# Spreading the norm factors of the attention heads by a store and a broadcast load in place of two matmuls

## The chip, the core and the metric

The kernel runs on one core of one Trainium2 chip. The time of a run is what the device reports for that core, in microseconds (us); smaller is better. A run of the kernel before takes 2206.67 us (median of three: 2206.53, 2206.67 and 2206.71).

## What is computed

One layer of a diffusion backbone over 2048 latent tokens of width 1024, with 256 context tokens: an adaLN-modulated RMSNorm, one input projection, differential attention in four heads beside a Fourier mixing of the other channels, an output projection with a gated residual, then a second norm, a two-level router and a mixture of 32 SwiGLU experts. What the change touches is the end of the attention. For each head the two softmax maps are subtracted, multiplied with the values, and each token's 128 outputs of that head are divided by their root mean square:

```python
p = jax.nn.softmax(s, axis=-1)
a = p[:, :, 0] - lam * p[:, :, 1]
return jnp.einsum('bhqk,bkhv->bqhv', a.astype(v.dtype), v)
...
o = lax.map(block, qb)
o = jnp.moveaxis(o, 0, 1).reshape(b, n, N_DA_HEADS, DA_V_DIM)
o = rms_norm(o, g_subln) * (1.0 - lambda_init)
```

The factor of this norm is one number for each token and head.

## The kernel before

The stages follow one another on the core: modulation, input projection, Fourier part, attention (`stage_attn`, L494), then router and experts (`stage_moe`). Attention works on 64 query tiles of 128 tokens (four heads of 16), and pairs of tiles `g` = 0 to 31 (256 tokens) share the matmuls with the values.

The order of the work in `stage_attn` is written out by hand. Time is cut into 384 slots, six to a query tile, so twelve to a pair; `put(s, order, f, ...)` (L651) files a function call under a slot, and the calls are issued slot by slot, within a slot by `order`. Every engine then takes its own instructions in that order. In slot `s` of tile `i` stand:

- `score` (L533): four matmuls of queries and 768 keys (L547) into one of two PSUM buffers `s`; VectorE scales them into SBUF and takes a running minimum (L550).
- `transp` (L598) of a tile two and a third tiles back: three transposes on TensorE (L606) into one of three PSUM buffers `tp`, which ScalarE and VectorE split into a high and a low part (`split`: L98 ScalarE, L99 VectorE).
- `av` (L610) of an earlier pair: the products of weights and values, three matmuls each (L103 to L105); 18 calls of it are spread over ten of a pair's twelve slots.
- the softmax around it: `expo` on ScalarE (L562); the sums and their ratio, `weight` (L569 GpSimd, L573 and L575 VectorE); `scale` of the second map in three parts (L582 ScalarE, L586 GpSimd, L584 VectorE); the sum of the two maps, `weigh` on GpSimd, three instructions to a tile (L590).

The head's norm is `norm(g, step)` (L617). Below, `s0` = 12 `g` + 32 is the slot of step 0.

- Step 0, slot `s0`: ScalarE copies the 128x256 product out of PSUM into `o` (L622; dimensions on partitions, tokens along the row) and squares it (L624); GpSimd starts the factor tile `r` (128 tokens x 2) (L628).
- Step 1, slot `s0 + 4`: two matmuls of the squares with ones (L634) put each token's sum on that token's partition, VectorE adds it (L636), GpSimd takes the power -1/2 (L637).
- Step 2, slot `s0 + 6`: the factors have to stand along the row, on every partition. Two matmuls with the identity spread them (L641) into a third use of the `tp` buffers, VectorE multiplies (L644), and the SP queue stores the tile `m` into the DRAM tensor `S.mix` (L646), which the output projection reads later.

The SP queue issues most of the DMAs, in program order, and a DMA that waits holds up those behind it: the four loads of a pair's queries (`load_queries`, L773, issued at L778), the store of `m`, and, once for each of heads 1 to 3, the keys and values of the next head (`load_head`, L756, at L762 and L767) 18 slots ahead of the head.

Steps 1 and 2 of pair 29, and all of pairs 30 and 31, are issued by a second list (`DRAIN`, L998) after slot 383.

Of the kernel before, what the change touches and what calls it, by code (L numbers as in the profile page):

```python
# [10 lines left out]
F32 = mybir.dt.float32  # L11
# [4 lines left out]
OP = mybir.AluOpType  # L16
# [3 lines left out]
N, D, NC = 2048, 1024, 256  # L20
NT, ND = N // 128, D // 128
KT = (N + NC) // 128
H, DH, VD = 4, 64, 128
# [99 lines left out]
def bcast(ap, parts=128):  # L123

    return bass.AP(tensor=ap.tensor, offset=ap.offset, ap=[[0, parts]] + list(ap.ap))
# [368 lines left out]
def stage_attn(tc, A, S, G, kv, head, q0, late):  # L494
    nc = tc.nc
    NQ = N // 128
# [6 lines left out]
    W2 = 2  # L503
    NV = 10
    N1 = 4
    XO, TO, AO, LO = 4, 3, 5, 6
    SE = ("act", "pool", "dve")
    LV = 2
    SC = DH ** -0.5
    with ExitStack() as outer, ExitStack() as ctx:  # L510
        sm = outer.enter_context(tc.tile_pool(name="sm", bufs=4, reuse_waits="tile"))
        ep = outer.enter_context(tc.tile_pool(name="ep", bufs=2, reuse_waits="tile"))
        ps = outer.enter_context(tc.tile_pool(name="aps", bufs=2, space=PSUM, reuse_waits="tile"))
# [3 lines left out]
        wk = ctx.enter_context(tc.tile_pool(name="awk", bufs=2, reuse_waits="tile"))  # L517
# [99 lines left out]
        def norm(g, step):  # L617
            if step == 0:
                t = K()
                O[g, 1] = t  # L620
                t.o = wk.tile([128, 256], F32, name="o")
                nc.scalar.activation(t.o, O[g], AF.Copy)  # L622
                t.sq = wk.tile([128, 256], F32, name="sq", bufs=1)
                nc.scalar.activation(t.sq, t.o, AF.Square)  # L624
                t.r = sm.tile([128, 2], F32, name="r")
                for j in range(2):
                    s0 = ST[2 * g + j][:, 14:15]
                    nc.gpsimd.tensor_scalar(t.r[:, j:j + 1], s0, s0, VD * EPS, op0=OP.mult, op1=OP.mult)  # L628
                return
            t = O[g, 1]  # L630
            if step == 1:
                t.p = ps.tile([128, 2], F32, name="tp", bufs=3)
                for j in range(2):
                    nc.tensor.matmul(t.p[:, j:j + 1], t.sq[:, j * 128:(j + 1) * 128], G.ones[:, 0:1],  # L634
                                     start=True, stop=True)
                nc.vector.tensor_add(t.r, t.r, t.p)  # L636
                nc.gpsimd.tensor_tensor(t.r, t.r, G.mhalf.to_broadcast([128, 2]), op=OP.pow)  # L637
            else:
                t.p = ps.tile([128, 256], F32, name="tp", bufs=3)
                for j in range(2):  # L640
                    nc.tensor.matmul(t.p[:, j * 128:(j + 1) * 128], t.r[:, j:j + 1].to_broadcast([128, 128]),  # L641
                                     G.ident, start=True, stop=True)
                t.m = wk.tile([128, 256], F32, name="m", bufs=1)
                nc.vector.scalar_tensor_tensor(t.m, t.o, G.gsub, t.p, op0=OP.mult, op1=OP.mult)  # L644
                h, b = divmod(g, NQ // 2)
                nc.sync.dma_start(S.mix[h, :, b * 256:(b + 1) * 256], t.m)  # L646

# [3 lines left out]
        def put(s, order, f, *a):  # L651
            at_slot.setdefault(s, []).append((order, f, a))
# [26 lines left out]
        for g in range(H * NQ // 2):  # L679
            s0 = 2 * NS * g + NS + LT + LV  # L680
            for j in range(KT):
                put(s0 + j * NV // KT, AO, av, g, j)
            s0 += NV
            put(s0, 3.5, norm, g, 0)
            put(s0 + N1, 5, norm, g, 1)
            put(s0 + N1 + 2, 5, norm, g, 2)

        def early(t):
            if t == 0:
# [20 lines left out]
        i, g = H * NQ - 1, H * NQ // 2 - 1  # L710
# [1305 lines left out]
def mkconst(tc, const):  # L2016
    nc = tc.nc
    G = K()
    G.pool = const
    G.ident = const.tile([128, 128], F32, name="ident")  # L2020
    make_identity(nc, G.ident)
    G.ones = const.tile([128, 128], F32, name="ones")
    nc.vector.memset(G.ones, 1.0)
    G.mhalf = const.tile([128, 1], F32, name="mhalf")
    nc.vector.memset(G.mhalf, -0.5)
    G.total = const.tile([128, NE], F32, name="total")
    G.order = const.tile([1, NE], I32, name="order")
    G.over = const.tile([1, 2, OVMAX], I32, name="over")
    G.perm = const.tile([NE, NE], F32, name="perm")
    G.before = const.tile([NE, NE], F32, name="before")  # L2030
    G.two = const.tile([NE, 2], F32, name="two")
    G.rk = const.tile([NE, 1], F32, name="rk")
    G.lead = const.tile([1, 1], I32, name="lead")
    G.nover = const.tile([1, 1], I32, name="nover")
    return G


def body(tc, A, out):
    nc = tc.nc
    S = K()  # L2040

    def dram(name, shape, dt=F32):
        return nc.dram_tensor(name, shape, dt, kind="Internal").ap()

    S.q, S.k = dram("q", [2, H, 2 * DH, N]), dram("k", [2, H, 2 * DH, KT * 128])
    S.v = dram("v", [2, KT, 128, 512])
    S.mix = dram("mix", [ND, 128, N])
    S.fd, S.frow = dram("fd", [2, 128, 3, 2, 512]), dram("frow", [1, 2, 256 + H])
    S.mod = dram("mod_rows", [1, 4 * D])
    S.x1, S.h2 = dram("x1", [N, D]), dram("h2", [N, D])  # L2050
    S.hold = dram("hold", [1, 1])
    S.list = dram("list", [NE * ROWS, 2], I32)
    with tc.tile_pool(name="const", bufs=1) as const:
        G = mkconst(tc, const)
        late = ExitStack()
        late.manual = late.enter_context(ExitStack())
        with tc.tile_pool(name="kv", bufs=1, reuse_waits="tile") as kv:
            with tc.tile_pool(name="ada", bufs=1) as ada, ExitStack() as top:
                pa = top.enter_context(tc.tile_pool(name="pa", bufs=1, space=PSUM, reuse_waits="tile"))
                P = Spectra(tc, A, S, kv)  # L2060
                first = top.enter_context(ExitStack())
                first.enter_context(tc.manual_schedule())
                x0 = stage_ada(tc, A, G, ada, pa, P)
                with tc.tile_pool(name="win", bufs=1, reuse_waits="tile") as wp, \
                        tc.tile_pool(name="raw", bufs=2, reuse_waits="tile") as raw:
                    P.wp = wp
                    P.mid = ada.tile([128, 2, 4, 2, H], F32R, name="mid")
                    P.manual = late.manual
                    stage_in(tc, A, S, G, wp, raw, P, first, x0)
                    top.close()  # L2070
                    head, q = stage_fourier(tc, A, S, G, wp, P)
            stage_attn(tc, A, S, G, kv, head, q, late)
        with late:
            stage_moe(tc, A, S, G, late, out)
    return S, G
# [34 lines left out]
```

## Time and profile before

| | us |
|---|---|
| median of three runs | 2206.67 |
| the profiled execution | 2205.05 |
| its span, first to last instruction | 2203.4 |
| one pair of query tiles (12 slots) in the steady part of attention | 20.34 |

The span is what the trace's clock counts from; all times of rows below are from its start. Attention lies at 473 to some 1165 us. Its pairs repeat with a period of 20.34 us; the steps from one L644 to the next have this length to 0.03 us from the second pair on, up to the drain.

How to read rows: PE is TensorE's matmuls, PEld its loading of weights (each matmul has one, and the loads run ahead beside the matmuls), DVE VectorE, ACT ScalarE, POOL GpSimd, SP the queue that issues DMAs. `out<-in` names tiles, `L12` is a line of the kernel. A bracket at the end of a timeline row tells how long the engine was idle before the instruction and whose result ended that.

### The profile page before, as it was taken

The numbers are of one execution on the slowest core, as the hardware profiler recorded it, in microseconds if no ns is written. First come the engines' busy times: TensorE is split into PE (matmuls) and PEld (weight loads), VectorE is DVE, ScalarE is ACT, GpSimd is POOL, SyncE is SP. The second block draws the span as 40 slices with busy tenths as digits, with TensorE's granted clock in tenths as the row PEclk, the third lists the DMA queues.
The fourth block names the chain that finished last, engine by engine and source line by source line (L and its number), as shares of the span: only waits on it lengthen the run. The fifth ranks groups of instructions, "written<-read, shape, count | busy, mean of one in ns | idle before, by whom it ended". The sixth has DMA issues, their size and how long they took to land. (4 is left out here: it accounts for less than half of the span.)

```text
span 2203.4 us, 35346 instructions
## 1 busy us (share of the span) xinstructions
PE 2091.4 (95%) x12607; PEld 1823.4 (83%) x12607; DVE 1813.7 (82%) x3644; ACT 1381.8 (63%) x2385; POOL 1016.9 (46%) x817
## 2 busy tenths in 40 slices
PE   6999999998999999999999999899999999999991
PEld 2877888778999999999988888888888888888871
DVE  5766654479999999999987878689888998989885
ACT  3734444258788888888872222466767767676663
POOL 2211121127787878888772433423444434544223
PEclk9999999999999999999999999999999999999996
DMA  7566543482151141243125443799999999999986
GB/s 261 202 199 204 187 142 112 169 230 36 30 117 37 41 106 37 50 100 111 28 87 172 153 137 128 250 291 311 311 312 317 317 325 322 319 322 309 316 301 278
DMA packets 265679, 423.02 MB, mean 192 GB/s; under 512 B 23618, under 2 KB 120904, under 8 KB 263706
## 3 DMA queue, kind: packets, MB, share of 16 engines
q1 hardware_dynamic: 240714, 362.91, 50.3%
q0 software_dynamic: 15872, 39.67, 7.1%
q10 hardware_dynamic: 8912, 18.14, 2.2%
q8 instruction: 100, 1.64, 0.3%
q14 instruction: 81, 0.66, 0.1%
HBM read 342.42 MB, written 84.17 MB: 194 GB/s over the span
## 5 line engine op out<-in xcount | busy, mean ns | idle before, releaser
L1703 DVE TENSOR_TENSOR wl<-mraw,wh 128x1024 fp32r<-128x1024 f32 x382 | 472.7, 1273 | 8.1 <-ACT wh L1699 8.0
L1699 ACT ACTIVATE wh<-mraw 128x1024 fp32r<-128x1024 f32 x384 | 382.4, 1049 | 74.0 <-DMA mraw<-in_w_up_dram 37.0
L550 DVE TENSOR_SCALAR_CACHE_REDUCE e<-s 128x768 f32<-128x768 f32 x384 | 364.7, 950 | 24.3 <-PE s L547 24.1
L590 POOL TENSOR_TENSOR e<-e,e 128x768 f32<-128x768 f32 x189 | 359.4, 1929 | 5.4 <-DVE e L584 0.5
L562 ACT ACTIVATE e<-e,st 128x1152 f32<-128x1152 f32 x256 | 320.3, 1251 | 11.1 <-DVE st L556 7.6
L1767 PE MATMUL mu<-mxt,wh 128*128 128x320 f32 (+2 forms) x1024 | 281.2, 354 | 0.9 <-DVE sg L1776 0.6
L1768 PE MATMUL mu<-mxt,wl 128*128 128x160 f32 (+2 forms) x1024 | 246.0, 240 | 0.0
L98 ACT ACTIVATE ath<-tp 128x384 fp32r<-128x384 f32 x384 | 186.2, 486 | 72.4 <-PE tp L606 70.8
L99 DVE TENSOR_TENSOR atl<-tp,ath 128x384 fp32r<-128x384 f32 x384 | 210.9, 550 | 2.2 <-ACT ath L98 2.0
L1847 POOL DMA_INDIRECT x<-my,idx x46 | 105.0, 2283 | 206.3 <-DVE my L1837 199.7
L1768 PEld LDWEIGHTS mu<-mxt,wl 128*128 128x128 f32 x1024 | 195.6, 191 | 0.7
L1767 PEld LDWEIGHTS mu<-mxt,wh 128*128 128x128 f32 x1024 | 192.2, 188 | 2.4 <-DVE sg L1776 0.9
L606 PE MATMUL tp<-ident,e 128*128 128x128 f32 x1152 | 188.1, 273 | 1.2 <-DVE e L595 1.2
L547 PE MATMUL s<-kB,q 128*128 128x384 f32 x768 | 170.8, 344 | 5.8 <-DVE e L550 5.8
L1730 POOL DMA_INDIRECT mx<-h,idx x48 | 62.9, 1311 | 217.2 <-DMA idx<-list 131.1
L606 PEld LDWEIGHTS tp<-ident,e 128*128 128x128 f32 x1152 | 149.2, 140 | 15.0 <-issue 1.6
L547 PE MATMUL s<-kA,q 128*128 128x384 f32 x672 | 150.4, 345 | 9.3 <-DVE e L550 9.2
L547 PEld LDWEIGHTS s<-kB,q 128*128 128x128 f32 x768 | 125.6, 188 | 9.1 <-DVE e L550 9.1
L547 PEld LDWEIGHTS s<-kA,q 128*128 128x128 f32 x672 | 110.3, 189 | 13.2 <-DVE e L550 13.1
L586 POOL TENSOR_TENSOR e<-e,st 128x896 f32<-128x896 f32 x63 | 105.9, 1681 | 27.9 <-DVE st L575 24.3
L118 POOL TENSOR_SCALAR ss<-ss 128x1 f32<-128x1 f32 x18 | 10.9, 607 | 232.7 <-ACT junk L116 224.1
L103 PE MATMUL py<-wh,mah 128*128 128x512 f32 (+1 forms) x264 | 106.6, 404 | 0.2
(517 smaller groups left out, 5703.1 us busy)
## 6 DMA issues: line engine op xcount, KB each, us to landing
mraw<-in_w_gate_dram SPq DMA_DIRECT2D x64, 1024.0 KB
mraw<-in_w_up_dram SPq DMA_DIRECT2D x64, 1024.0 KB
mraw<-in_w_down_dram SPq DMA_DIRECT2D x64, 1024.0 KB
raw<-in_w_ada_dram SPq DMA_DIRECT2D x16, 1024.0 KB
q<-q SPq DMA_DIRECT2D x120, 128.0 KB
v<-z SPq DMA_DIRECT2D x18, 512.0 KB
k<-z SPq DMA_DIRECT2D x18, 512.0 KB
boot<-in_w_ada_dram SPq DMA_DIRECT2D x8, 1024.0 KB
```

The costliest lines, as they stand in the source:

```text
L98: nc.scalar.activation(hi, src, AF.Copy)
L99: nc.vector.tensor_sub(lo, src, hi.bitcast(F32))
L103: nc.tensor.matmul(out, ah, bh, start=start, stop=False)
L547: nc.tensor.matmul(p[:, u, :hw], q[:, m, x, qs], kvt.k[m][:, k0:k0 + hw], start=x == 0, stop=x == 1)
L550: nc.vector.tensor_scalar(E[i][m][:, c * CH:(c + 1) * CH].rearrange("p (u k) -> p u k", u=2), p[:, :, :hw], -SC, None, op0=OP.mult, op1=OP ...
L562: nc.scalar.activation(e, e, AF.Exp, scale=-1.0, bias=st[:, 6 + m:7 + m], accum_out=st[:, 8 + 2 * u + m:9 + 2 * u + m])
L590: nc.gpsimd.tensor_add(E[i][0][:, ks], E[i][0][:, ks], E[i][1][:, ks])
L606: nc.tensor.transpose(p[:, u, :], E[i][0][:, k0:k0 + 128], G.ident)
L1699: nc.scalar.activation(W.h[:, us, :], W.raw[:, us, :], AF.Copy)
L1703: engine.tensor_sub(W.l[:, us, :], W.raw[:, us, :], W.h[:, us, :].bitcast(F32))
L1767: nc.tensor.matmul(p[:, i, :2 * n], h, B.t[:, d, :], start=d == 0, stop=False)
L1768: nc.tensor.matmul(p[:, i, :n], l, B.t[:, d, :n], start=False, stop=d == ND - 1)
```

## The change

For pairs 0 to 27 (`g < LATE`) the factors take another way. Step 1 stores `r` into a new DRAM tensor `S.rn` (256 factors, by token) and loads that row back into a tile `m` on all 128 partitions, both on the SP queue. Step 2 stands at `s0 + 15`, nine slots later than before, has no matmuls, and multiplies `o` with `m` in place. The tile `o` has three buffers in place of two. Pairs 28 to 31 are computed as before.

```diff
@@ -503,6 +503,8 @@
     W2 = 2
     NV = 10
     N1 = 4
+    N2 = 11
+    LATE = H * NQ // 2 - 4
     XO, TO, AO, LO = 4, 3, 5, 6
     SE = ("act", "pool", "dve")
     LV = 2
@@ -618,7 +620,7 @@
             if step == 0:
                 t = K()
                 O[g, 1] = t
-                t.o = wk.tile([128, 256], F32, name="o")
+                t.o = wk.tile([128, 256], F32, name="o", bufs=3)
                 nc.scalar.activation(t.o, O[g], AF.Copy)
                 t.sq = wk.tile([128, 256], F32, name="sq", bufs=1)
                 nc.scalar.activation(t.sq, t.o, AF.Square)
@@ -635,13 +637,20 @@
                                      start=True, stop=True)
                 nc.vector.tensor_add(t.r, t.r, t.p)
                 nc.gpsimd.tensor_tensor(t.r, t.r, G.mhalf.to_broadcast([128, 2]), op=OP.pow)
+                if g < LATE:
+                    t.m = wk.tile([128, 256], F32, name="m", bufs=1)
+                    nc.sync.dma_start(S.rn[g].rearrange("(j p) -> p j", j=2), t.r)
+                    nc.sync.dma_start(t.m, bcast(S.rn[g]))
             else:
-                t.p = ps.tile([128, 256], F32, name="tp", bufs=3)
-                for j in range(2):
-                    nc.tensor.matmul(t.p[:, j * 128:(j + 1) * 128], t.r[:, j:j + 1].to_broadcast([128, 128]),
-                                     G.ident, start=True, stop=True)
-                t.m = wk.tile([128, 256], F32, name="m", bufs=1)
-                nc.vector.scalar_tensor_tensor(t.m, t.o, G.gsub, t.p, op0=OP.mult, op1=OP.mult)
+                if g < LATE:
+                    factors = t.m
+                else:
+                    factors = ps.tile([128, 256], F32, name="tp", bufs=3)
+                    for j in range(2):
+                        nc.tensor.matmul(factors[:, j * 128:(j + 1) * 128],
+                                         t.r[:, j:j + 1].to_broadcast([128, 128]), G.ident, start=True, stop=True)
+                    t.m = wk.tile([128, 256], F32, name="m", bufs=1)
+                nc.vector.scalar_tensor_tensor(t.m, t.o, G.gsub, factors, op0=OP.mult, op1=OP.mult)
                 h, b = divmod(g, NQ // 2)
                 nc.sync.dma_start(S.mix[h, :, b * 256:(b + 1) * 256], t.m)
 
@@ -683,7 +692,7 @@
             s0 += NV
             put(s0, 3.5, norm, g, 0)
             put(s0 + N1, 5, norm, g, 1)
-            put(s0 + N1 + 2, 5, norm, g, 2)
+            put(s0 + N1 + (N2 if g < LATE else 2), 5, norm, g, 2)
 
         def early(t):
             if t == 0:
@@ -2046,6 +2055,7 @@
     S.v = dram("v", [2, KT, 128, 512])
     S.mix = dram("mix", [ND, 128, N])
     S.fd, S.frow = dram("fd", [2, 128, 3, 2, 512]), dram("frow", [1, 2, 256 + H])
+    S.rn = dram("rn", [H * N // 256, 256])
     S.mod = dram("mod_rows", [1, 4 * D])
     S.x1, S.h2 = dram("x1", [N, D]), dram("h2", [N, D])
     S.hold = dram("hold", [1, 1])
```

## Rows read from the trace of the kernel before

**Rows 1.** Page of the profile, part 1: busy time, share of the span, instructions.

```profile
PE 2091.4 (95%) x12607; PEld 1823.4 (83%) x12607; DVE 1813.7 (82%) x3644; ACT 1381.8 (63%) x2385; POOL 1016.9 (46%) x817
```

**Rows 2.** Busy time by stretch: length, engines, PEclk (granted clock), DMA share, GB/s.

```profile
541.90:562.30 20.40, 17.19 (x114) 16.28 (x112) 19.61 (x51) 13.42 (x25) 11.15 (x13) 0.92 0.02 7
...
806.60:827.00 20.40, 20.04 (x148) 19.40 (x148) 19.50 (x51) 17.69 (x34) 16.43 (x14) 1.00 0.11 33
```

**Rows 3.** Waits, 600 to 1100 us: total us, times, longest.

```profile
DVE e L550 <- PE s L547: 20.7, 75, 0.3
```

**Rows 4.** Timeline of PEld, 819 to 842 us: start, us, engine, instruction.

```profile
819.87 0.65 PEld L547 LDWEIGHTS s<-kA,q 128*128 128x128 f32 x4 [0.57 <-DVE e L550]
...
823.79 0.65 PEld L547 LDWEIGHTS s<-kA,q 128*128 128x128 f32 x4
...
824.82 0.53 PEld L641 LDWEIGHTS tp<-ident,r 128*128 128x128 f32 x4
...
825.62 0.66 PEld L547 LDWEIGHTS s<-kA,q 128*128 128x128 f32 x4
...
832.59 0.66 PEld L547 LDWEIGHTS s<-kA,q 128*128 128x128 f32 x4
...
833.98 0.66 PEld L547 LDWEIGHTS s<-kA,q 128*128 128x128 f32 x4
...
840.21 0.65 PEld L547 LDWEIGHTS s<-kA,q 128*128 128x128 f32 x4 [0.57 <-DVE e L550]
```

**Rows 5.** Timeline of DVE, 800 to 842 us.

```profile
817.36 1.12 DVE L584 TENSOR_SCALAR e<-e,st 128x768 f32<-128x768 f32 x1
...
818.87 0.94 DVE L550 TENSOR_SCALAR_CACHE_REDUCE e<-s 128x768 f32<-128x768 f32 x1
...
820.21 0.94 DVE L550 TENSOR_SCALAR_CACHE_REDUCE e<-s 128x768 f32<-128x768 f32 x1
...
821.55 0.14 DVE L556 TENSOR_REDUCE st<-st 128x1 f32<-128x3 f32 x1
...
825.88 0.22 DVE L575 SCALAR_TENSOR_TENSOR st<-st,lam 128x1 f32<-128x1 f32 x1
...
826.48 0.47 DVE L644 SCALAR_TENSOR_TENSOR m<-o,gsub,tp 128x256 f32<-128x256 f32 x1
...
826.87 0.15 DVE L556 TENSOR_REDUCE st<-st 128x1 f32<-128x3 f32 x1
...
827.81 0.62 DVE L584 TENSOR_SCALAR e<-e,st 128x768 f32<-128x768 f32 x1
```

**Rows 6.** Timeline of POOL, short windows, so that nothing is merged.

```profile
816.38 1.68 POOL L586 TENSOR_TENSOR e<-e,st 128x896 f32<-128x896 f32 x1
...
820.12 1.83 POOL L590 TENSOR_TENSOR e<-e,e 128x768 f32<-128x768 f32 x1
...
826.18 1.68 POOL L586 TENSOR_TENSOR e<-e,st 128x896 f32<-128x896 f32 x1 [0.79 <-DVE st L575]
```

**Rows 7.** Timeline of DVE in the drain: two operands in SBUF.

```profile
1135.10 3.21 DVE L595 SCALAR_TENSOR_TENSOR e<-e,st,e 128x768 f32<-128x768 f32 x1
```

**Rows 8.** Timeline of POOL beside it, short windows.

```profile
1135.11 2.38 POOL L1050 TENSOR_TENSOR kB<-kA,e 128x1024 fp32r<-128x1024 f32 x1
...
1137.45 3.10 POOL L1050 TENSOR_TENSOR kB<-kA,e 128x1024 fp32r<-128x1024 f32 x1
```

**Rows 9.** Timeline of the SP queue: start, us to issue.

```profile
605.62 19.77 SPq L778 DMA_DIRECT2D q<-q  x4
...
1154.25 0.38 SPq L1066 DMA_DIRECT2D vA<-in_g_ffn_norm_dram  x1
...
1163.41 2.82 SPq L646 DMA_DIRECT2D mix<-m  x2
```

**Rows 10.** Timeline of DVE where it waits for such DMAs.

```profile
1159.78 1.23 DVE L1068 TENSOR_TENSOR kA<-kA,vA 128x1024 f32<-128x1024 f32 x1 [2.85 <-DMA vA<-in_g_ffn_norm_dram]
...
1165.39 0.48 DVE L644 SCALAR_TENSOR_TENSOR m<-o,gsub,tp 128x256 f32<-128x256 f32 x1 [0.81 <-DMA mix<-m]
```

## The prediction

> **What bounds the kernel now.** I read the page's busy times first: TensorE is busy 95% of the span, VectorE 82%, ScalarE 63%, GpSimd 46% [rows 1]. That is a mean over stages, so the next view was the busy time by stretch, around the lines that change. In a pair of the steady part (20.40 us) the weight loads fill 19.40 us and VectorE 19.50 us at a granted clock of 1.00, with the DMA engines at 11% [rows 2]: two engines lie within a hair of each other, and neither is the bound by its share alone. Which one ends waits has to be read in order of time.
>
> The timeline of weight loads shows the loop. TensorE stands still once in a pair, 0.57 us, for VectorE's L550, and starts the next slot's scores at 819.87; the same happens at 840.21, so a pair is 20.34 us [rows 4]. From 819.87 to the scores at 832.59 TensorE never waits for 0.1 us or more, and in that stretch VectorE waits for it: 20.7 us of such waits in the 500 us from 600 to 1100, which is 24.6 pairs, so 0.84 us per pair [rows 3]. After 832.59 VectorE runs without such a wait, through the L584 that takes 1.12 us (its counterpart of this pair starts at 817.36 [rows 5]), up to the L550 whose end lets TensorE go at 840.21. The loop of one pair is thus 12.7 us of TensorE and some 7.6 us of VectorE. What is taken from TensorE between 819.87 and 832.59 shortens it, if VectorE keeps up there; what is taken from TensorE elsewhere only lengthens its 0.57 us.
>
> **The change, part by part.**
>
> *The two matmuls go (L641).* They start at 824.82, inside TensorE's part of the loop. A slot that holds them and one value product takes from 823.79 to 825.62, 1.83 us; one with a value product and no L641 takes from 832.59 to 833.98, 1.39 us [rows 4]. So 0.44 us per pair. The third use of the `tp` buffers goes too; no wait for such a buffer stands in the steady pairs, so I cost that at nothing. There are 28 changed pairs. In the first, TensorE has time over: in the start-up stretch the weight loads fill 16.28 of 20.40 us and VectorE 19.61 [rows 2]. That leaves 27 pairs.
>
> *The product moves nine slots (L644).* It leaves the place where it took 0.39 us of VectorE's time (826.48 to the L556 at 826.87) and goes ahead of the L556 that starts at 821.55 [rows 5]. Both places lie in TensorE's part of the loop, so VectorE's own part keeps its length. Two things change beside the place.
>
> First, its second operand was in PSUM and is now in SBUF like the first. The nearest rows of a product with two operands in SBUF beside a busy GpSimd are in the drain: L595 on 768 columns, started at 1135.10, took 3.21 us and ended at 1138.31, which is 0.82 us after the GpSimd instruction started at 1135.11 had ended (1137.49); the GpSimd instruction behind that took 3.10 us in place of 2.38 [rows 7, 8]. So the product waits for the GpSimd instruction in progress, gets in at its end, and holds up the next one. At the new place GpSimd runs L590 from 820.12 to 821.95 [rows 6]: the product comes at 821.55, waits 0.40 us, and then runs 256/768 of the 0.82, some 0.27 us; it ends at 822.22 and, with the 0.08 us that neighbours overlap (0.47 us long, 0.39 us apart [rows 5]), takes 0.59 us of VectorE's time. The ends are 0.39 (no block) and 2.05 (a whole L590 of 1.83 us first). I take 0.59 because the phase is rigid: both the L590 and VectorE's path to 821.55 run without waits from the end of the L584 that started at 817.36, which itself ends 0.42 us after GpSimd's L586 (818.48 against 818.06 [rows 5, 6]).
> The Trainium skill, "SBUF — State Buffer", section "Who interferes with whom", has this as a rule and it speaks against the change: a VectorE instruction with two SBUF inputs and a GpSimd instruction that reads SBUF exclude each other, and the later one blocks until the earlier has ended; one with a single SBUF input does not contend. The rows of the drain agree. Without that rule the product would cost 0.39 and the sum below would be the same, since TensorE's part sets it.
>
> Second, at the old place less lies between L575 and L584. L586 on GpSimd starts when L575 is done and holds till 827.86 (826.18 and 1.68 [rows 6]); L584, now 0.39 us earlier, comes at 827.42 and, by the 0.42 us above, ends at 828.28 and not at 828.43 [rows 5]. So 0.15 of the 0.39 is won there.
>
> *VectorE's account.* It gets 0.59 and gives 0.15, so 0.44 more per pair, in a stretch that shrinks by 0.44: it needs 0.88 us of slack and has 0.84 of waits plus the tail of about 0.08 that each of its three waits hides. Between 0.00 and 0.04 us per pair is lost; I take 0.43 us won of the 0.44. This is a tie: every further tenth on VectorE costs a tenth of the pair.
> The later L556 delays ScalarE's exponential behind it by some 0.6 us; ScalarE idles 2.7 us of the pair [rows 2], and the splits behind it are due later on VectorE too, so I cost that at nothing.
>
> *The two DMAs (SP).* The factors are there by 824.82, where L641 read them, and the product now wants them at 841.89 (821.55 and a period): 17.1 us. A store of 128 KB issued at 1163.41 let its buffer go at 1165.39, 2.0 us; a broadcast load of 512 KB, issued at 1154.25, was waited for until 1159.78, 5.5 us with what lay ahead of it [rows 9, 10]. The store of the factors is smaller (1 KB, though in single elements) and the load is 128 KB, so 7.5 us is an upper price and 0 the lower, both under cover; if the cover is gone, VectorE stands. The load also waits for the one buffer `m`, free some 2 us after the previous product, so about when the store has landed. Behind these waits on SP stand the next head's loads and, nine slots later than before, the store of `m` and the four query loads; the queries are used a full pair later, and nothing reads `S.mix` before the drain. The tightest place is a head's load, three times: there the four query loads took 19.77 us to issue, to 625.39 [rows 9]. The factors' store now stands behind them: 625.4 and 7.5 make 632.9, and the product of that pair is due at 638.5 (602.74, 623.08 and so on are the old places, and the new one is 15.4 us behind). 5.6 us are left. The third buffer of `o` costs no instruction.
>
> **The sum.** 27 pairs by 0.43 us make 11.6 us. The profiled execution is 2205.05 us, so it becomes 2193.4; the median of the runs shown is 1.6 us above it, and I carry the difference over: 2206.67 - 11.6 = **2195.1 us**. The stages behind start when attention ends and move up as a whole; nothing of them was under way before.
>
> **Rivals.**
> *VectorE takes over.* If the blocked product or the shifted L584 costs 0.1 to 0.35 us more than above, the pair is VectorE's and 0.08 to 0.33 us are won: 2198 to 2204, some 2201. For: the tie. Against: VectorE's busy time counts overlaps, so its true slack is somewhat larger.
> *The saving is swallowed.* If TensorE waits as much longer elsewhere (its 0.57 us grows to 1.0), as in the first pair [rows 2], the time stays at 2206, give or take 2. Against: L641 lies in the unbroken stretch.
> *The port turns it round.* If GpSimd's third L590 gets in ahead of the product, or the product comes just behind 821.95, it waits through another L590 of 1.83 us: VectorE is 1.8 us over its tie and the pair becomes 19.9 + 1.8 = 21.7, 1.4 us longer than now, by 27: 2244 us. It decides from about 0.45 us of further waiting on, where the won 0.43 is gone. For: the skill's rule says that the block lasts for the whole instruction. Against: in the drain the product got in between two GpSimd instructions that stood back to back [rows 7, 8].
> *The factors land late.* From 17.1 us for both DMAs on, VectorE waits in every pair; at a head's load from 13.1 us on, three times. The second costs a few us, 2198 to 2200.
>
> **How the numbers follow.** The forecast has 0.62, VectorE taking over (with late factors at the heads) 0.15, the swallowed saving 0.10, the port or late factors in every pair 0.13. A measurement of this kernel can tell 0.2%, 4.4 us. Faster by more holds the forecast and three quarters of the second case: 0.73; slower 0.14, of which 0.01 is from the third case; the rest, 0.13, is the same. The range begins at 28 pairs by 0.44 with 1.5 us of scatter, 2192, and takes in the second case and the near part of the third up to 2205, which leaves some 0.2 out.
>
> **What would show it.** Right: a period of 19.9 us from product to product; no L641 ahead of pair 28; L644 some 0.7 us long, starting 0.4 us before a GpSimd L590 ends, and that engine's next L590 about 0.3 us longer; the L584 of the slot behind L575 at 0.85 in place of 0.62; no wait of L644 for a DMA; PE's wait for L550 still near 0.57. Wrong: L644 of 2 us or more, a DMA as its releaser, VectorE without waits for scores, or a period of 20.3.

## The result, and the profile after

The changed kernel takes 2226.09 us (median of six runs, 2220.8 to 2236.6) against 2206.69 us before: a ratio of 1.0095, 95% interval 1.0081 to 1.0108. It is slower by some 19 us, where 2195.1 was forecast. The profiled execution after took 2226.60 us, 21.6 us more than the one before. In attention, the 28 pairs from the 37th slot to the 373rd grow from 574.4 to 595.2 us together, so 20.8 us of the loss lie there.

Line numbers move: L644 is now L653, L547 is L549, L550 is L552, L575 is L577, L584 is L586, L590 is L592; the store of the factors is L642, their load L643, the store of the product L655.

**The steady pairs do what was forecast.** Two rows of the weight loads, as in [rows 4]:

```profile
663.42 0.65 PEld L549 LDWEIGHTS s<-kB,q 128*128 128x128 f32 x4 [0.57 <-DVE e L552]
...
683.30 0.65 PEld L549 LDWEIGHTS s<-kB,q 128*128 128x128 f32 x4 [0.56 <-DVE e L552]
```

The distance is 19.88 us in place of 20.34, and TensorE's one wait is still 0.56 to 0.57 us. On VectorE, the product and the L586 behind L577, which answer to [rows 5]:

```profile
684.98 0.69 DVE L653 SCALAR_TENSOR_TENSOR m<-o,gsub,m 128x256 f32<-128x256 f32 x1
...
691.00 0.86 DVE L586 TENSOR_SCALAR e<-e,st 128x768 f32<-128x768 f32 x1
```

The product is 0.69 us long (0.47 before), the L586 0.86 (0.62 before). GpSimd beside them, which answers to [rows 6]:

```profile
683.56 1.83 POOL L592 TENSOR_TENSOR e<-e,e 128x768 f32<-128x768 f32 x1
...
685.35 2.02 POOL L592 TENSOR_TENSOR e<-e,e 128x768 f32<-128x768 f32 x1
```

The product comes at 684.98, 0.41 us before the L592 ends at 685.39, and the next L592 takes 2.02 in place of 1.85 us. So it waits for the instruction in progress, gets in at the seam, and holds up the next by 0.17 us.

**The loss stands at three places.** The waits of VectorE, and of the SP queue, over attention (us in total, times, longest), which answer to [rows 3]:

```profile
DVE e L552 <- PE s L549: 5.5, 22, 0.7
...
DVE m L653 <- DMA m<-rn: 28.5, 3, 10.1
...
SPq L643 <- DMA rn<-r: 217.2, 28, 10.3
```

VectorE waits 5.5 us for scores, 23.7 us in the same stretch before, so it is now nearly the bound itself, the tie of the prediction. The product waits for its factors only three times, 28.5 us together: in pairs 4, 12 and 20, whose step 1 follows the load of the next head's keys and values. The last line says why it is not one or two us: in each of the 28 pairs the load of the factors waits 7.8 us on average for their store. The SP queue at the first head (start, time to issue), in the place of [rows 9]:

```profile
599.52 0.54 SPq L642 DMA_DIRECT2D rn<-r  x1
...
607.69 0.33 SPq L643 DMA_DIRECT2D m<-rn  x1
...
608.11 1.24 SPq L771 DMA_DIRECT2D kB<-k  x2
...
609.44 1.09 SPq L776 DMA_DIRECT2D vB<-v  x1
...
616.39 13.51 SPq L655 DMA_DIRECT2D mix<-m  x1
...
630.03 2.53 SPq L787 DMA_DIRECT2D q<-q  x4
...
633.00 0.38 SPq L642 DMA_DIRECT2D rn<-r  x1
...
640.49 0.33 SPq L643 DMA_DIRECT2D m<-rn  x1
```

Here is the chain. The factors' store of pair 3 is issued at 599.52, and their load waits for it until 607.69. Only then can the head load go, at 608.11; before it went at 603.66. Behind its 4.7 MB stands, new, the product's store of pair 3: it comes at 616.39 and takes 13.51 us to issue. Behind it the queries of the next pair, the first of the new head, and behind those, at 633.00, the factors' store of pair 4, whose load can go 7.5 us later, at 640.49. Two engines are late by it:

```profile
636.26 1.62 PE L549 MATMUL s<-kB,q 128*128 128x384 f32 x4 [2.75 <-DMA q<-q]
...
644.41 0.48 DVE L653 SCALAR_TENSOR_TENSOR m<-o,gsub,m 128x256 f32<-128x256 f32 x1 [8.80 <-DMA m<-rn]
```

The product of pair 4 could have started at 635.6 and stands 8.80 us. TensorE stands first for something else: the new head's first scores start 2.75 us late, for want of their queries (2.7 and 2.1 us at the other two heads). VectorE, which needs these scores, stands longer still for its factors, so the late queries cost nothing here; but they are a second thing that the block makes late. TensorE then computes two slots of scores and stands again until VectorE goes on. Its clock falls. Busy time by stretch (length; PE, PEld, DVE, ACT, POOL; granted clock; DMA share, GB/s), in the place of [rows 2]:

```profile
636.00:644.00 8.00, 7.27 (x30) 6.90 (x30) 0.00 (x0) 0.49 (x1) 1.68 (x1) 0.57 0.07 18
...
645.00:665.00 20.00, 18.75 (x124) 18.03 (x124) 18.81 (x46) 17.20 (x32) 14.06 (x12) 0.91 0.22 40
...
665.00:685.00 20.00, 19.65 (x144) 19.01 (x144) 19.80 (x50) 17.23 (x33) 16.53 (x14) 1.00 0.21 41
```

TensorE had stood 2.75 us for the queries; in the 8 us behind that its granted clock is 0.57, so mostly the lower of its two levels, 1.2 GHz, in the pair behind 0.91, and then 1.00, the upper one of 2.4 GHz, again. The account of the 28 pairs: the three stalled ones are 28.5, 29.8 and 29.4 us long and those behind them 20.9, 21.4 and 21.6, together 29.7 us above six pairs of 20.34; the 20 undisturbed ones win 20 by 0.45 or 9.0. That makes 20.7 of the 20.8 us.

### The profile page after: what moved, and what is told of

The parts are those of the page before. It is cut to its first block, busy times and chain, and to the rows that moved or that the text cites. A ratio compares the mean times of both kernels' runs of the same rounds, so it can differ in the third digit from the quotient of the medians.

```text
span 2225.0 us, 35210 instructions
## 1 busy us (share of the span) xinstructions
PE 2092.3 (94%) x12495; PEld 1823.6 (82%) x12495; DVE 1820.9 (82%) x3644; ACT 1368.8 (62%) x2385; POOL 1016.7 (46%) x817
## 5 line engine op out<-in xcount | busy, mean ns | idle before, releaser
L552 DVE TENSOR_SCALAR_CACHE_REDUCE e<-s 128x768 f32<-128x768 f32 x384 | 363.0, 946 | 8.5 <-PE s L549 6.7
L592 POOL TENSOR_TENSOR e<-e,e 128x768 f32<-128x768 f32 x189 | 360.0, 1932 | 5.4 <-DVE e L586 0.5
L549 PE MATMUL s<-kB,q 128*128 128x384 f32 x768 | 174.4, 349 | 19.2 <-DVE e L552 14.3
L549 PE MATMUL s<-kA,q 128*128 128x384 f32 x672 | 152.4, 349 | 17.1 <-DVE e L552 14.3
L549 PEld LDWEIGHTS s<-kB,q 128*128 128x128 f32 x768 | 128.2, 192 | 22.8 <-DVE e L552 19.9
L549 PEld LDWEIGHTS s<-kA,q 128*128 128x128 f32 x672 | 111.8, 191 | 21.4 <-DVE e L552 18.4
```

Of the source, the lines that this page charges most:

```text
L549: nc.tensor.matmul(p[:, u, :hw], q[:, m, x, qs], kvt.k[m][:, k0:k0 + hw], start=x == 0, stop=x == 1)
L552: nc.vector.tensor_scalar(E[i][m][:, c * CH:(c + 1) * CH].rearrange("p (u k) -> p u k", u=2), p[:, :, :hw], -SC, None, op0=OP.mult, op1=OP ...
L592: nc.gpsimd.tensor_add(E[i][0][:, ks], E[i][0][:, ks], E[i][1][:, ks])
```

## The experiments

**Head pairs as before.** Pairs 4, 12 and 20 go back to the two matmuls.

```diff
+        def spread(g):
+            return g < LATE and g % 8 != 4
...
-                if g < LATE:
+                if spread(g):
...
-            put(s0 + N1 + (N2 if g < LATE else 2), 5, norm, g, 2)
+            put(s0 + N1 + (N2 if spread(g) else 2), 5, norm, g, 2)
```

> Pairs 4, 12 and 20, whose step 1 falls behind the load of the next head, spread their factors by the two matmuls again, two slots after step 1; all other pairs as in the changed kernel. If the loss is the three waits of the product for its factors (8.8 to 10.1 us each, with a slower pair behind each), it is gone: the three pairs take 20.3 us, the other pairs stay at 19.9, and the run takes 2206.7 - 23 x 0.45 = 2196, between 2194 and 2199. If the head loads only hand the wait on to the pair behind (5, 13, 21), or the loss is one of the later stages, it stays above 2206.

Measured: 2245.18 us, ratio 1.0176 (1.0158 to 1.0193): worse than the changed kernel. That is above the 2206 of the second expectation, but not for its reason: no wait went to pairs 5, 13 and 21. The SP queue and VectorE at the first head:

```profile
619.73 13.98 SPq L658 DMA_DIRECT2D mix<-m  x1
...
633.83 2.53 SPq L790 DMA_DIRECT2D q<-q  x4
```

```profile
617.82 1.88 DVE L656 SCALAR_TENSOR_TENSOR m<-o,gsub,m 128x256 f32<-128x256 f32 x1 [0.54 <-DMA m<-rn]
...
639.14 0.48 DVE L656 SCALAR_TENSOR_TENSOR m<-o,gsub,tp 128x256 f32<-128x256 f32 x1 [14.95 <-DMA mix<-m]
```

The product of pair 3 comes at 617.82, and its store takes 13.98 us to issue behind the head load. Pair 4's product, early again, needs the one tile `m` that this store still reads, and stands 14.95 us (14.4 and 13.2 us at the other two heads). So taking away the two small DMAs behind the head load isn't enough: what the move has put behind the head load is the product's store of the pair ahead. The experiment was confounded by the single buffer, which I had left out of account.

**Clear of the heads.** The same edit, with the pair ahead of each head load taken out too:

```diff
+            return g < LATE and g % 8 not in (3, 4)
```

> Pairs 3, 4, 11, 12, 19 and 20 keep the two matmuls and the early product; the other 22 are spread. The order on SP around the three head loads is then that of the kernel before. The steady gain alone is left: no wait of a product over 2.5 us, the spread pairs at 19.9 us, and 2206.7 - 21 x 0.45 = 2197, between 2195 and 2200. If the gain of the steady pairs is given back in the experts' stage or in the drain, it stays above 2203.

Measured: 2196.81 us, ratio 0.9954 (0.9937 to 0.9970), as expected. No product waits for a store or a load of factors in the loop, and pair 3 stores its product ahead of the head load again:

```profile
603.02 0.33 SPq L658 DMA_DIRECT2D mix<-m  x1
...
603.39 1.71 SPq L774 DMA_DIRECT2D kB<-k  x2
```

It differs from the experiment above only in pairs 3, 11 and 19 (and 27, which no head load follows, so 21 pairs are spread, not 22). The 48 us between the two are theirs: a factors' store that the head load waits for, a store of the product that slides behind the head load, and the one buffer behind that. What is left against the kernel before is the gain of the pairs away from the heads.

**Head pairs alone.** The reverse: only pairs 4, 12 and 20 are spread.

```diff
+            return g in (4, 12, 20)
```

> Only pairs 4, 12 and 20, the three whose products waited, are spread by store and load; all others are as in the kernel before. So no factors' store stands ahead of the head load on SP, and no product's store between the head load and the queries: the head load starts near 603.7 us and the four query loads are issued by 625.5, as before. If the order on SP made the loss, the factors' store is issued at 625.5 and lands in 8 us, the load in 4: 637.5 against 638.5 us where the product is due, a wait under 1.5 us in each of the three, and attention as long as before to 4 us. If a head load and two small DMAs do not fit together in any order, the three waits are 8 to 10 us again and the run is some 30 us slower than before.

Measured: 2209.29 us (one run), beside 2207.68 before, and the 28 pairs take 577.7 us in place of 574.4. SP and VectorE at the first head:

```profile
605.19 1.22 SPq L774 DMA_DIRECT2D kB<-k  x2
...
607.15 19.88 SPq L790 DMA_DIRECT2D q<-q  x4
...
627.12 0.54 SPq L645 DMA_DIRECT2D rn<-r  x1
...
636.17 0.34 SPq L646 DMA_DIRECT2D m<-rn  x1
```

```profile
640.30 1.75 DVE L656 SCALAR_TENSOR_TENSOR m<-o,gsub,m 128x256 f32<-128x256 f32 x1 [0.66 <-DMA m<-rn]
```

The head load goes at 605.19, the queries directly behind it, as before the change, and the factors' store at 627.12: with the old order on the queue the factors land 0.66 us late in place of 8.80. So the order on SP makes about eight of the nine us, and the first expectation holds: the three waits are 0.66, 0.45 and 0.44 us. Both changes of the order count. From the start of the same slot, the 73rd, the head load goes 5.8 us later here and 11.6 us later in the changed kernel, where it has to wait for the factors' store of pair 3; and from the head load to the factors' store of pair 4 it is 21.9 us here and 24.9 us there, with the product's store between. The product is 1.75 us long here: it came at 640.30, 0.36 us after an L592 of 1.84 us had started on GpSimd, and ended 0.27 us after it. That is the price of a missed seam.

**The head load in two.**

```diff
-            KV[h], values = load_head(nc, S, kv, h)
-            values()
+            KV[h], V[h] = load_head(nc, S, kv, h)
+
...
+        def next_values(h):
+            V[h]()
...
-            put(h * NQ * NS - 3 * NS, 0, next_head, h)
+            put(h * NQ * NS - 5 * NS, 0, next_head, h)
+            put(h * NQ * NS - 3 * NS, 0, next_values, h)
```

> All pairs spread by store and load; a head's keys are loaded 30 slots ahead of it and its values 18, in place of both 18 slots ahead. If what hurts is the length of one block of 4.7 MB on the queue (22 us against a cover of 17 us), two blocks of some 11 to 13 us fit under the cover: no wait of the product over 2 us, 2206.7 - 25 x 0.45 = 2195.5, between 2194 and 2200. If any head load ahead of the two small DMAs makes them late, there are six waits in place of three, and the time stays above 2210.

Measured: 2211.97 us, ratio 1.0023 (1.0008 to 1.0037). The product's waits:

```profile
DVE m L657 <- DMA m<-rn: 16.0, 7, 4.1
```

Seven waits of 16.0 us in place of three of 28.5, the longest 4.1. Six of them are at the head loads, two to each, as the second expectation has it, and the time is above its 2210, though not by much; the seventh, 0.48 us, is in pair 25, far from any head load. The first expectation fails, but the sum of the waits shows that the length of the block counts; half a block still does not fit.

**The product a pair later.** Two buffers for `m`, and 20 us more cover.

```diff
-    N2 = 11
+    N2 = 23
...
-                    t.m = wk.tile([128, 256], F32, name="m", bufs=1)
+                    t.m = wk.tile([128, 256], F32, name="m", bufs=2)
```

> The product stands 23 slots behind step 1 in place of 11 (one whole pair later, in the same slot of a pair) and the factor tile has two buffers. The store, the load and the head loads stay where they are. If the cover was only too short at the heads, 20 us more of it hide the waits of 8.8 to 10.1 us: every pair from the second on takes 19.9 us, 2206.7 - 27 x 0.45 = 2194.5, between 2193 and 2198. If the queue falls further and further behind after a head, or another wait takes the place (the output tile's buffers), it stays above 2203.

Measured: 2215.85 us, ratio 1.0033 (1.0014 to 1.0053). The product no longer waits for its factors, but the next thing on the queue is late. SP at the first head, and the wait it makes:

```profile
613.72 1.23 SPq L771 DMA_DIRECT2D kB<-k  x2
...
615.04 0.61 SPq L776 DMA_DIRECT2D vB<-v  x1
...
620.36 15.30 SPq L655 DMA_DIRECT2D mix<-m  x1
...
635.75 2.53 SPq L787 DMA_DIRECT2D q<-q  x4
```

```profile
PE s L549 <- DMA q<-q: 4.5, 1, 4.5
```

The product's store takes 15.30 us behind the head load, and the queries behind it are issued at 635.75, too late for the scores of the new head. A wait has taken the place of a wait: the one that in the changed kernel stood 2.75 us, hidden behind the product's. It is not all of the loss. In the profiled execution the 28 pairs take 577.8 us, 3.4 more than before, and the stretch from the last slot's VectorE instruction to the last product takes 46.1 us in place of 40.2: with 23 slots the product of pair 27 falls into the drain.

**Queries first, and the product a pair later.** The same kernel, with the new head's first queries loaded ahead of its keys and values (pair 27 goes back to matmuls, out of the drain's way).

```diff
-    LATE = H * NQ // 2 - 4
+    LATE = H * NQ // 2 - 5
...
-            if i % 2 == 0 and c == 0 and 1 < i // 2 + 1 < H * NQ // 2:
+            if i % 2 == 0 and c == 0 and 1 < i // 2 + 1 < H * NQ // 2 and (i // 2 + 1) % 8:
...
+            put(h * NQ * NS - 3 * NS - 1, 0, load_q, h * NQ // 2)
             put(h * NQ * NS - 3 * NS, 0, next_head, h)
```

> As the kernel with the product a pair later and two buffers for the factors, with two edits: the queries of a new head's first pair are loaded one slot ahead of that head's keys and values in place of six slots behind, and pair 27 is spread by matmuls, so that its product is out of the way of the drain. There the waits of the product were gone, and scores waited for queries in their place (4.5 us at the first head). If that order is all that is left, the pairs at the heads take 19.9 us too, and the run takes 2206.7 - 26 x 0.45 = 2195, between 2193 and 2199. If another load behind the head load is late next, it stays above 2201.

Measured: 2196.27 us, ratio 0.9944 (0.9923 to 0.9965), as expected; this kernel beats both the changed one and the one before. SP and the weight loads at the first head:

```profile
610.55 2.53 SPq L788 DMA_DIRECT2D q<-q  x4
...
617.58 17.13 SPq L655 DMA_DIRECT2D mix<-m  x1
...
634.81 0.37 SPq L642 DMA_DIRECT2D rn<-r  x1
...
644.28 0.32 SPq L643 DMA_DIRECT2D m<-rn  x1
```

```profile
654.97 0.65 PEld L549 LDWEIGHTS s<-kB,q 128*128 128x128 f32 x4 [0.57 <-DVE e L552]
...
674.88 0.65 PEld L549 LDWEIGHTS s<-kB,q 128*128 128x128 f32 x4 [0.58 <-DVE e L552]
```

The block is as long as ever (the product's store takes 17.13 us, the factors' store 9.5), yet what stands behind it now has a whole pair to spare, and the pair behind the head is 19.91 us long. The profiled execution is 23.0 us shorter than that of the kernel with the product a pair later: 12.9 us in the 28 pairs, where the queries count, and 6.6 us from the last slot to the last product, where of the edits only the return of pair 27 to matmuls can; most of the rest, 3.9 us, lies ahead of attention, where no edit is.

**Queries first alone.** The loads of the queries alone are moved, on the changed kernel: N2, the buffers and LATE stay.

```diff
-            if i % 2 == 0 and c == 0 and 1 < i // 2 + 1 < H * NQ // 2:
+            if i % 2 == 0 and c == 0 and 1 < i // 2 + 1 < H * NQ // 2 and (i // 2 + 1) % 8:
...
+            put(h * NQ * NS - 3 * NS - 1, 0, load_q, h * NQ // 2)
```

> The changed kernel with one edit: the queries of a new head's first pair are loaded one slot ahead of that head's keys and values. The product stays 11 slots behind step 1, with one factor tile. The same bytes stand ahead of the factors' store, since the queries only change places with the head load, so if the product's wait at a head is the time that the queue needs for them, the store is issued within 1 us of where it was, the three waits stay at 8 to 10 us and the run takes 2220 to 2227: neither this edit nor the later product alone, but both together take the loss away. If the 2.5 us of issuing the four query loads behind the block are the point, each wait is 2.5 to 3.5 us shorter, and the run takes 2214 to 2219.

Measured: 2231.39 us, ratio 1.0117 (1.0092 to 1.0142): the edit alone wins nothing, and the time lies somewhat above the expected band. SP at the first head:

```profile
611.32 2.54 SPq L788 DMA_DIRECT2D q<-q  x4
...
619.39 16.23 SPq L655 DMA_DIRECT2D mix<-m  x1
...
636.04 0.38 SPq L642 DMA_DIRECT2D rn<-r  x1
...
645.32 0.32 SPq L643 DMA_DIRECT2D m<-rn  x1
```

The factors' store of pair 4 goes at 636.04, 3.0 us later than in the changed kernel by the clock; but the whole run is 3.0 us later there (the factors' store of pair 3 goes at 602.50 against 599.52), so relative to the work it stands where it stood. The query loads that went ahead hold up the head load instead (613.95 against 608.11, so 2.9 us by the work). The store then takes 9.3 us to let its load go (636.04 to 645.32) in place of 7.5, and the product stands 10.9 us in place of 8.80 (10.9 and 8.4 us at the other heads). Changing places with the queries brings nothing as long as the same bytes lie ahead of the factors.

**Pieces of the store.** Two factors side by side, 128 pieces of 8 bytes in place of 256 of 4; the factors then stand in another order, so the attention's output and the experts' work differ, and only attention is read.

```diff
-                    nc.sync.dma_start(S.rn[g].rearrange("(j p) -> p j", j=2), t.r)
+                    nc.sync.dma_start(S.rn[g].rearrange("(p j) -> p j", j=2), t.r)
```

> The store writes the two factors of a partition side by side (128 pieces of 8 bytes in place of 256 of 4), so that the factors stand in another order and the output is not the reference's. The queue waits 7.8 us on average from this store to the load behind it. If the number of pieces sets that time, it falls to 4 to 5 us, the three waits of the product shrink by about as much, and the run takes 2210 to 2218. If it is the landing of any such store, whatever its pieces, the 7.8 us and the 2226 stay.

Measured: 2304.57 us as a whole, which says nothing here (the experts' stage grew, on other data). In attention:

```profile
SPq L643 <- DMA rn<-r: 113.3, 28, 5.8
...
DVE m L653 <- DMA m<-rn: 9.7, 3, 4.0
```

113.3 us in 28 waits are 4.0 us each, in place of 7.8, and the product's three waits shrink from 28.5 to 9.7 us, so by 6.3 us each. That is more than the 3.7 of one store, because two factors' stores lie in that chain: from the issue of the store to that of its load, the one of pair 3 takes 5.05 us (600.68 to 605.73) in place of 8.17, and the one of pair 4 takes 4.35 (631.42 to 635.77) in place of 7.49, together 6.3 less. The same 28 pairs take 572.1 us, against 595.2 with the small pieces and 574.4 before. So about half of the time that the load waits for this store is the price of its pieces; the run changes their number and their size together and does not tell the two apart.
The Trainium skill, "DMA: Bandwidth & Descriptors", section "Rules for kernel authors", says that a last dimension that isn't contiguous becomes one descriptor per element and should be rearranged. The packets under 512 bytes between 520 and 1160 us agree: beyond the 7072 of the kernel before, the changed kernel has 281 more to each of the 28 pairs, this one 160, so 121 fewer for 128 pieces fewer. The size is 3.7 us for 128 pieces.

**The factors on another queue.** Store and load are issued from ScalarE's queue, two and seven slots behind step 1.

```diff
-                    nc.sync.dma_start(S.rn[g].rearrange("(j p) -> p j", j=2), t.r)
-                    nc.sync.dma_start(t.m, bcast(S.rn[g]))
+            elif step == 3:
+                nc.scalar.dma_start(S.rn[g].rearrange("(j p) -> p j", j=2), t.r)
+            elif step == 4:
+                nc.scalar.dma_start(t.m, bcast(S.rn[g]))
...
+            if g < LATE:
+                put(s0 + N1 + 2, 0, norm, g, 3)
+                put(s0 + N1 + 7, 9, norm, g, 4)
```

> All 28 pairs as in the changed kernel, but the store and the load of the factors are issued from ScalarE's queue, two and seven slots behind step 1, so that SP holds only the head loads, the queries and the stores of the products. If the loss is the order on SP (the head load waits there for the factors' store, and the product's store, the queries and the next factors stand behind 4.7 MB), the head load starts 6 to 10 us earlier, no product and no scores wait over 1 us, and the run takes 2206.7 - 26 x 0.45 = 2195, between 2192.5 and 2198. If it is the 16 DMA engines that are full, whatever the queue, the factors of pairs 4, 12 and 20 are still some 8 us late and the time is above 2215. If ScalarE's own time for two more DMAs (0.9 us a pair) counts, all pairs are 0.3 to 0.9 us longer and the time is 2203 to 2218.

Measured: 2216.20 us, ratio 1.0037 (1.0024 to 1.0050). ScalarE's queue, SP and VectorE at the first head:

```profile
599.36 0.39 ACTq L643 DMA_DIRECT2D rn<-r  x1
...
610.33 0.33 ACTq L645 DMA_DIRECT2D m<-rn  x1
```

```profile
600.05 1.22 SPq L776 DMA_DIRECT2D kB<-k  x2
...
601.51 1.31 SPq L781 DMA_DIRECT2D vB<-v  x1
```

```profile
622.46 0.48 DVE L655 SCALAR_TENSOR_TENSOR m<-o,gsub,m 128x256 f32<-128x256 f32 x1 [5.63 <-DMA m<-rn]
```

The head load goes at 600.05, 8 us earlier, as expected. But now pair 3's factors, whose load is issued at 610.33 from a queue of its own, need 12.1 us beside the head load, to 622.46, and 3.9 us when nothing is beside them (640.49 to 644.41 in the changed kernel); the product stands 5.63 us (5.8 and 4.5 us in pairs 11 and 19, and 1.7 us in pair 24). So the order on SP is not all: the small load beside 4.7 MB is slow from ScalarE's queue too. Of the 32 us that the heads cost in the changed kernel (six pairs by 19.89 as the measure) some 22.5 remain here. The second expectation comes nearest, with the time above 2215, but the late factors are those of pairs 3, 11 and 19, and by 5 us, not 8; the third has the time in its range too, but the pairs away from the heads take 19.9 us, so ScalarE's time for the two DMAs is not what costs.
The Trainium skill, "DMA: Bandwidth & Descriptors", section "Issuing engines are not separate DMA queues", says that DMAs of all issuing engines run on the same 16 engines and interleave, so that another queue saves only issue time. The 12.1 us agree with the first half. The second half falls short here: on SP a DMA that waits holds up those behind it, and without the factors' store there the head load goes 8 us earlier, so the other queue saves a wait and not only the issue.

## Why the prediction was wrong

**The bound, right.** The loop of TensorE's part and VectorE's part, and that the two matmuls lie in TensorE's part: 0.45 to 0.46 us per pair were won, where 0.43 of 0.44 was the term.

**The product's new place, right.** The wait for GpSimd's instruction in progress (0.69 us measured, 0.67 forecast), the seam, the next L592 held up (by 0.17 us, where about 0.3 was forecast), the L586 at 0.86 (0.86 forecast): all stand in the trace. The rival of the missed seam is real too, 1.75 us in the head pairs alone, but did not come up in the steady pairs, as the rigid phase said.

**The two DMAs: the step that failed.** Away from the heads the cover held: some 8 and 4 us against 17.1. The step was "the tightest place is a head's load", with the factors' store at 625.4 and 5.6 us to spare. Four terms of it were wrong.
First, the order on the queue. I counted the queries behind the head load, and forgot there the store of the previous product, which the nine slots move from ahead of the head load to behind it, and the head load's own wait for the factors' store ahead of it. The store of pair 4's factors was issued at 633.0 and not at 625.4. The head pairs alone, with the old order, show it: 0.66 us late and not 8.80. "The queries are used a full pair later" fails at the heads for the same reason: they were issued at 630.0 and TensorE stood 2.75 us for them.
Second, the price of two DMAs. The 7.5 us, taken as an upper price from a whole 128 KB store and a broadcast load, was what the store of the factors alone took: 256 single elements took longer than 128 KB in rows, 7.5 us against 2.0. With the load at 3.9 us it was 11.4. The case with larger pieces shows this. I had written that it goes out in single elements, and priced it by the nearest large store all the same.
Third, the place where the product is due. By the trace after, it was ready at 635.6 and not at 638.5: attention starts 1.3 us earlier in that execution, and what the spread pairs ahead save, 0.45 us each, I had not taken off. The three together make 7.6 + 3.9 + 2.9 = 14.4 us, which turns the 5.6 us to spare into the 8.8 us of the first wait.
Fourth, the price of being late. "A few us, 2198 to 2200" for three events was 8.8 to 10.1 us of waiting each, and 1.0 to 1.7 us more in the pair behind, where the clock comes back (0.91 at the first head); that the clock is all of these 1.0 to 1.7 us is not shown. The rival was named, with its place, but it shared the 0.15 of VectorE taking over and counted as faster than before, because its margin had been worked out with the first three errors.

**The saving, right, and outweighed:** 9.0 us won in the undisturbed pairs against 29.7 lost at the heads.

What is open: whether a split head load with larger pieces would fit under eleven slots; it wasn't tried.

## What to carry to other kernels

When a DMA is moved in the program, write down the whole order of its queue around the largest transfer, before and after, with what each entry waits for: here a store that nobody waited for slid behind a 4.7 MB load and pushed two things that were waited for. Price a store by its pieces, not its bytes, and give a chain of two dependent DMAs cover for the sum of them beside the largest transfer, not in the quiet stretch. If a wait goes away by more cover, look at once for what is late next on the same queue; here it took two edits together. The later product alone won about 10 of the 30 us that both won over the changed kernel, the earlier queries alone none.

## What the runs showed of the hardware that was not expected

- A store of 1 KB in 256 pieces of 4 bytes held up the load behind it for 7.8 us on average, in 128 pieces of 8 bytes for 4.0; a store of 128 KB in the kernel before let its buffer go in 2.0 us.
- An issue on SP behind the head load stood in the queue itself, 13.2 to 17.1 us for one store in the runs with the small pieces and the head load in one (10.2 to 10.8 us with the larger pieces), so that everything behind it stood too.
- A 128 KB broadcast load took 3.9 us alone and 12.1 us beside the head load, issued from ScalarE's queue.
